# A hybrid retention and attention layer: convolution constants loaded during the retention, rotation and output gate of the retention on VectorE

## The chip, the cores and the metric

The kernel runs on one core of one Trainium2 chip. A core has a matrix engine (TensorE, PE in the views, with its weight loads as PEld), three engines for elementwise work (VectorE as DVE, ScalarE as ACT, GpSimd as POOL) and an engine that here only issues transfers (SyncE, SP). Each engine carries out its own list of instructions in order and waits on semaphores for the others; transfers are issued by an engine (rows of SPq, POOLq) and carried out by 16 DMA engines. The metric is device time of one execution in microseconds, lower is better.

## The reference

One step of a diffusion backbone with one layer, for 128 context tokens and 512 latent tokens, D_MODEL 1024, all in float32. The parts that the change touches are the retention branch (rotation of q and k, retention, normalisation, output gate) and the constants of the convolution in the feed-forward part:

```python
def rope_1d(x, pos):
    half = x.shape[-1] // 2
    ...
    x1 = x[..., :half].astype(jnp.float32)
    x2 = x[..., half:].astype(jnp.float32)
    return jnp.concatenate([x1 * cos - x2 * sin, x2 * cos + x1 * sin], axis=-1).astype(x.dtype)

def retention_branch(rq, rk, rv, rg, pos, dec_f, dec_b, s0_f, s0_b):
    B, L, _ = rq.shape
    q = rope_1d(rq.reshape(B, L, R_HEADS, R_DK).transpose(0, 2, 1, 3), pos)
    k = rope_1d(rk.reshape(B, L, R_HEADS, R_DK).transpose(0, 2, 1, 3), pos) * (R_DK ** -0.5)
    v = rv.reshape(B, L, R_HEADS, R_DV).transpose(0, 2, 1, 3)
    ...
    o_f, s_f = retention_scan(q, k, v, lg_f, s0_f)
    o_b, s_b = retention_scan(q[:, :, ::-1], k[:, :, ::-1], v[:, :, ::-1], lg_b, s0_b)
    o = rms_scale(o_f + o_b[:, :, ::-1])
    o = o.transpose(0, 2, 1, 3).reshape(B, L, RET_V)
    return jax.nn.silu(rg.astype(jnp.float32)) * o, s_f, s_b

def token_mixer(h, w_in, ...):
    z = h @ w_in
    q, k, v, rq, rk, rv, rg, ga, gr = jnp.split(z, ...)
    ...
    ya = attend_blocks(q, k_all, v_all)
    yr, s_f, s_b = retention_branch(rq, rk, rv, rg, ret_pos, dec_f, dec_b, s0_f, s0_b)
    y = jax.nn.sigmoid(ga) * (ya @ w_att_o) + jax.nn.sigmoid(gr) * (yr.astype(h.dtype) @ w_ret_o)
    return y @ w_out, (k, v, s_f, s_b)

def conv_ffn(h, w_up, conv_w, conv_b, w_down):
    u = h @ w_up
    up = jnp.pad(u, ((0, 0), (1, 1), (0, 0)))
    uc = conv_w[0] * up[:, :L] + conv_w[1] * up[:, 1:L + 1] + conv_w[2] * up[:, 2:L + 2] + conv_b
    a, g = jnp.split(uc, 2, axis=-1)
    return (jax.nn.silu(g) * a) @ w_down
```

The layer: conditioned normalisation, then attention and retention side by side on the same input, gates and one output projection, a second conditioned normalisation and the feed-forward part, a last normalisation.

## The kernel before

**Tiles and number format.** The 640 tokens are 5 tiles of 128: t=0 is the context, t=1 to 4 are latents. A float32 matmul is made of three with a reduced format (mm3, L156 to L159): both operands are split into a high part and the rest, and high x high, high x rest and rest x high are added in PSUM. A weight of 1 MB comes into one of two buffers `raw` by a transfer on the SP queue (w_raw, L132 to L134). Then w_split (L137) makes its parts by 1024 columns: ACT casts the high part (L145), DVE subtracts it from the raw weight (L150). The parts lie in a ring of eight buffers `wh`.

**Groups.** a_group (L173) computes 512 columns for all five tiles: five PSUM banks (`mm.N`), two halves of four blocks of rows, and after the second half of a tile its evac function takes the bank over. A new group can start in a bank only when the old content has been copied out.

**Order.** The scheduler of the language orders the instructions of each engine from the program text and the dependencies; it is free to put a transfer far ahead of the text around it. In some stretches the order is fixed by hand (manual_schedule). So a row of the SP queue may stand earlier than its line suggests.

**The front.** After the normalisation of the input, the keys and values of all tiles are computed (z_kv, L432) into five banks; kv_hi and kv_lo (L337 to L340) split their weight. evac_kv (L565 to L575) copies the banks out, on ACT (L566) and DVE (L571). The group of the queries follows (evac_q, L628 to L639); its weight's halves are raw.11 and raw.16, and its first matmul writes mm.16, into the bank of mm.11. The convolution constants `cw`, 4 x [128, 44] elements (three taps and a bias for 44 blocks of 128 channels), are loaded in L754 to L756 of the program text, in the attention; each of these transfers has 5632 packets of one element of 4 bytes. cw is used first in conv (L1358), in the feed-forward part.

**The retention's projections.** RK, RQ and RV are groups (L864) whose steps are interleaved with mod_rest (L243 to L303), which computes further conditioning vectors on ACT (L290) and DVE (L292). evac_rqk (L851) handles a tile of RK or RQ: ACT copies the bank to z (L854), then the rotation multiplies the swapped halves of z with the sines (two multiplies of 128x256 on POOL, L858), z with the cosines (L860, DVE) and adds both (L861, DVE). Tiles of RK are in `ret.u5.5`, of RQ in `ret.u4.4`, the swapped product in `r2k`, a ring of buffers that many helpers share.

**The retention.** retention (L978) goes over ten pairs (t, hh) of tile and half of the heads, in three steps one pair apart: ret_a transposes q and k on PE and copies them out (kt is `ret2.rkT`, L944); DVE scales the queries by the decays there (L939); ret_b makes the scores, which DVE multiplies with the decay mask (L955); ret_c multiplies with the values and keeps the result and its squares' sums (L970). When a half is done, ret_d (L972) takes the roots and multiplies all five tiles on POOL (L976). Between these steps run the steps of the gate's first group, rg0 (L1002); the second follows behind. evac_rg (L993) makes the gate of a tile: tanh on ACT (L996), one DVE operation (L997), and the multiply of the retention's result, 128x512, on POOL (L999). Behind it the merge begins, whose first gate weight is raw.131 (L1192).

Of the kernel before, what the change touches and what calls it, by code (L numbers as in the profile page):

```python
# [70 lines left out]
def hybrid_step(ctx: ExitStack, tc: tile.TileContext, a: dict, o: dict):  # L71
    nc = tc.nc
# [369 lines left out]
    with tc.manual_schedule(engines={ET.PE, ET.DVE, ET.Activation}):  # L442
# [308 lines left out]
        for _ in range(n):  # L751
            next(fill, None)
    qts[1] = qT_head(1)
    for i in range(3):  # L754
        nc.sync.dma_start(cw[:, i, :], a["conv_w"][0, i].rearrange("(c p) -> p c", p=P))
    nc.sync.dma_start(cw[:, 3, :], a["conv_b"][0].rearrange("(c p) -> p c", p=P))  # L756
# [94 lines left out]
    def evac_rqk(i):  # L851
        def f(t, ps):
            z = rqk[i][:, t, :].rearrange("p (h d) -> p h d", h=8)
            nc.scalar.copy(z.rearrange("p h d -> p (h d)"), ps)  # L854
            sw = r2k().rearrange("p (h d) -> p h d", h=8)
            for b in range(2):
                xs = z[:, :, (1 - b) * 32:(2 - b) * 32]
                nc.gpsimd.tensor_mul(sw[:, :, b * 32:(b + 1) * 32], xs,  # L858
                                     r1[:, t, 1:2, b * 32:(b + 1) * 32].to_broadcast([P, 8, 32]))
            V.tensor_mul(z, z, r1[:, t, 0:1, :].to_broadcast([P, 8, 64]))  # L860
            V.tensor_add(z, z, sw)  # L861
        return f
# [109 lines left out]
    def ret_d(hh):  # L972
        rso = rsqrt(rs2, sso[:, hh].rearrange("p t h -> p (t h)"), 4 * NT, 1.0 / P, post=0.5)
        for t in range(NT):
            ov = rvv[hh][:, :, t, :]
            nc.gpsimd.tensor_mul(ov, ov, rso[:, 4 * t:4 * t + 4].unsqueeze(2).to_broadcast([P, 4, P]))  # L976
# [16 lines left out]
    def evac_rg(g):  # L993
        def f(t, ps):
            th = r2k()
            nc.scalar.activation(th, ps, AF.Tanh, scale=0.5)  # L996
# [2 lines left out]
            nc.gpsimd.tensor_mul(ov, ov, th.rearrange("p (h d) -> p h d", h=4))  # L999
# [782 lines left out]
```

## Time and profile before

| | us |
|---|---|
| median of three runs | 1158.55 (1156.24, 1159.28, 1158.55) |
| profiled execution, whole | 1157.51 |
| its span, first to last instruction | 1155.7 |
| busy in the span: DVE, ACT | 832.4, 599.4 |
| mean granted TensorE clock | 0.995 of full |

What lies between span and time of the profiled execution is 1.81 us, around the instructions. A slice of the page's second part is 28.9 us wide. Its rows give the busy share of each engine in tenths:

```
PE   5979999999999999999999999999999999999996
DVE  4556777677968966453747738979777598589878
POOL 0042110000012410043002223011112111121012
PEclk9989999999999999999999999999999999999999
```

Busy time says where an engine works. Whether its work sets the time is told by the waits of the engine that is always busy, and by the chain of what released what. In the rows quoted below a group has its busy time in us and the mean of one in ns, then the idle time of the engine ahead of it and what ended it.

### The profile page before, as it was taken

To read this page: it belongs to the slowest core of one execution; us is meant where nothing else is said; L and a number is where in the kernel's file an instruction comes from. 1 tells how busy PE (TensorE), PEld (TensorE's weight loads), DVE (VectorE), ACT (ScalarE), POOL (GpSimd) and SP (SyncE) were. 2 spreads that over 40 slices of the span, in tenths; PEclk is the share of its full clock that TensorE was granted. 3 is DMA by queue.
4 is the path that set the end of the run, shared out by engine and by line. 5 is a ranking of instruction groups with operands and counts; after the bars stand their busy time and mean duration, and the time that the engine had idled before them with its cause. 6 is when DMAs were issued, how large, how long until landed. Compare 5 with 4: busy or idle time off the path is not lost.

```text
span 1155.7 us, 17472 instructions
## 1 busy us (share of the span) xinstructions
PE 1118.4 (97%) x6725; PEld 1007.7 (87%) x6725; DVE 832.4 (72%) x1434; ACT 599.4 (52%) x1127; POOL 190.2 (16%) x210
## 2 busy tenths in 40 slices
PE   5979999999999999999999999999999999999996
PEld 4768899999988778888999988999899899899995
DVE  4556777677968966453747738979777598589878
ACT  5345656554232425552435536668657567475463
POOL 0042110000012410043002223011112111121012
PEclk9989999999999999999999999999999999999999
DMA  9952210015765442111116947456657656666462
GB/s 311 199 151 73 73 37 23 16 37 180 262 209 168 141 147 92 37 37 37 44 67 134 297 144 199 118 144 124 134 126 160 163 94 165 129 126 163 120 127 110
DMA packets 132611, 147.92 MB, mean 128 GB/s; under 512 B 27160, under 2 KB 101992, under 8 KB 132272
## 3 DMA queue, kind: packets, MB, share of 16 engines
q1 hardware_dynamic: 103152, 115.59, 31.3%
q0 software_dynamic: 29104, 31.10, 17.0%
q8 instruction: 53, 0.87, 0.3%
q14 instruction: 30, 0.25, 0.1%
q10 hardware_dynamic: 272, 0.11, 0.0%
HBM read 115.05 MB, written 8.67 MB: 107 GB/s over the span
## 4 chain that ended last, share of the span: by engine, by line
PE 78%; DVE 10%; ACT 5%; issue 3%; DMA 2%; POOL 1%; ACTq 0%; DVEq 0%; SPq 0%; POOLq 0%
DVE mod.acc.24_3630 L292 1%; DMA weights.raw.414_10655<-in_w_down 1%; DVE x1.u1.1_6298 L1454 1%; DMA mod.wm.31_3814<-in_w_mod 1%; DMA p1q.u1.1_598<-in_k_norm_g 0%; DMA weights.raw.247_7694<-in_w_down 0%; POOL f0.s.5_3423 L976 0%; DVE ret.u4.4_3425 L861 0%; DMA const.u2.2_72<-in_b_mod 0%; DVE ret.u4.4_3425 L860 0%; DVE x1.u1.1_6298 L1503 0%; DVE x1.u1.1_6298 L1466 0%; PE mm1.mm.16_711 L157 0%; DVE weights.raw.395_10304 L1551 0%; DVE x1.u1.1_6298 L1261 0%
## 5 line engine op out<-in xcount | busy, mean ns | idle before, releaser
L817 POOL DMA_DIRECT2D spill.u2.2_2895<-f1.s.1_1160 x1 | 0.6, 597 | 129.8 <-DVE mod.u3.3_2850 L602 129.8
L1106 POOL DMA_DIRECT2D weights.wh.164_5833<-weights.raw.156_5766 x1 | 1.3, 1342 | 69.5 <-DVE f1.s.9_5177 L1145 69.5
L1591 DVE TENSOR_TENSOR t7.u4.4_6786<-t7.u4.4_6786,const.u1.1_70 128x320 f32<-128x320 f32 x10 | 4.9, 492 | 10.1 <-ACT const.u1.1_70 L1590 10.1
L913 DVE SCALAR_TENSOR_TENSOR ret2.u1.1_4178<-ret2.u1.1_4178,const.u11.11_86 64x128 f32<-64x128 f32 x24 | 6.8, 338 | 6.4 <-ACT ret2.u1.1_4178 L906 6.3
L915 DVE SCALAR_TENSOR_TENSOR ret2.u1.1_4178<-ret2.u1.1_4178,const.u11.11_86 64x128 f32<-64x128 f32 x24 | 6.6, 381 | 4.7 <-ACT ret2.u1.1_4178 L908 4.7
L582 POOL TENSOR_TENSOR p1.u1.1_604<-p1.u3.3_608,p1q.u1.1_598 128x512 f32<-128x512 f32 x1 | 1.3, 1289 | 50.7 <-DMA p1.u3.3_608<-in_rope 50.7
L150 DVE TENSOR_TENSOR weights.wh.113_4368<-weights.raw.111_4365,weights.wh.112_4367 128x1024 fp32r<-128x1024 f32 x1 | 1.2, 1226 | 10.4 <-ACT weights.wh.112_4367 L145 10.4
L157 PE MATMUL mm1.mm.16_711<-weights.wh.12_718,acts.u1.1_90 128*128 128x512 f32 x2 | 1.4, 698 | 7.2 <-ACT p1.u4.4_610 L566 7.2
L150 DVE TENSOR_TENSOR weights.wh.18_789<-weights.raw.16_786,weights.wh.17_788 128x1024 fp32r<-128x1024 f32 x1 | 1.2, 1226 | 9.8 <-ACT weights.wh.17_788 L145 9.8
L860 DVE TENSOR_TENSOR ret.u5.5_3426<-ret.u5.5_3426,ret.u1.1_3419 128x512 f32<-128x512 f32 x5 | 3.5, 690 | 6.6 <-POOL ret.r2k.6_3541 L858 2.8
L427 ACT CAST acts.u1.1_90<-f0.s.2_104 128x640 fp32r<-128x640 f32 x4 | 2.9, 728 | 9.5 <-DVE f0.s.2_104 L425 9.5
L976 POOL TENSOR_TENSOR f0.s.5_3423<-f0.s.5_3423,ret2.ny20.13_4764 128x512 f32<-128x512 f32 x5 | 6.0, 1236 | 8.0 <-DVE ret2.ny20.13_4764 L220 8.0
L157 PEld LDWEIGHTS mm1.mm.16_711<-weights.wh.12_718,acts.u1.1_90 128*128 128x128 f32 x2 | 0.6, 309 | 7.7 <-ACT p1.u4.4_610 L566 7.6
L551 ACT ACTIVATE f0.s.3_710<-f0.s.3_710,p1q.ny20.11_878 128x128 f32<-128x128 f32 x20 | 6.0, 388 | 2.5 <-DVE p1q.ny20.11_878 L218 2.5
L444 PE MATMUL aux1.aux.1_134<-const.u1.1_70,const.u2.2_72 80*128 80x80 f32 x1 | 0.4, 368 | 7.0 <-DMA const.u2.2_72<-in_b_mod 7.0
L1498 POOL TENSOR_TENSOR x1.u1.1_6298<-x1.u1.1_6298,weights.raw.422_10855 128x512 f32<-128x512 f32 x3 | 4.9, 1629 | 12.7 <-ACT x1.tm.111_10868 L1471 9.8
L145 ACT CAST weights.wh.67_3288<-weights.raw.66_3286 128x1024 fp32r<-128x1024 f32 x1 | 1.1, 1056 | 11.3 <-PE mm3.mm.8_3129 L196 11.3
L145 ACT CAST weights.wh.77_3520<-weights.raw.76_3518 128x1024 fp32r<-128x1024 f32 x1 | 1.1, 1056 | 11.2 <-PE mm3.mm.16_3386 L196 11.2
L427 ACT CAST acts.u1.1_90<-f0.s.1_103 128x640 fp32r<-128x640 f32 x4 | 2.9, 726 | 7.5 <-DVE f0.s.1_103 L425 7.4
L145 ACT CAST weights.wh.17_788<-weights.raw.16_786 128x1024 fp32r<-128x1024 f32 x1 | 1.0, 1045 | 11.0 <-DMA weights.raw.16_786<-in_w_in 11.0
L1108 DVE TENSOR_TENSOR weights.wh.152_5685<-weights.raw.151_5631,weights.wh.152_5685 128x512 fp32r<-128x512 f32 x1 | 0.7, 696 | 8.3 <-ACT weights.wh.152_5685 L1099 8.3
L1465 DVE TENSOR_TENSOR x1.u1.1_6298<-x1.u1.1_6298,gate.u1.1_6284 128x512 f32<-128x512 f32 x10 | 6.7, 681 | 0.0
(6898 smaller groups left out, 4968.0 us busy)
## 6 DMA issues: line engine op xcount, KB each, us to landing
spill.u1.1_2894<-x1.u1.1_6298 POOLq DMA_DIRECT2D x5, 512.0 KB, 3.6
xin.u1.1_102<-in_x_sample SPq DMA_DIRECT2D x4, 512.0 KB, 4.8
p0.u5.5_119<-in_w_mod SPq DMA_DIRECT2D x2, 1024.0 KB, 10.0
p0.u6.6_125<-in_w_mod SPq DMA_DIRECT2D x2, 1024.0 KB, 14.8
p0.u7.7_128<-in_w_mod SPq DMA_DIRECT2D x2, 1024.0 KB, 12.3
gate.u1.1_6284<-spill.u3.3_2896 SPq DMA_DIRECT2D x2, 1024.0 KB, 4.8
x1.u1.1_6298<-in_x_sample SPq DMA_DIRECT2D x4, 512.0 KB, 8.9
out_y_sample<-x1.u1.1_6298 SPq DMA_DIRECT2D x8, 256.0 KB, 2.0
```

Of the source, the lines that this page charges most:

```text
L145: nc.scalar.copy(hi, rv)
L292: V.scalar_tensor_tensor(d, ws[n], sc, d, op0=ALU.mult, op1=ALU.add)
L427: nc.scalar.copy(hT[0][:, k, :], xk)
L551: nc.scalar.activation(x[:, j], x[:, j], AF.Copy, scale=rstd[:, j:j + 1])
L860: V.tensor_mul(z, z, r1[:, t, 0:1, :].to_broadcast([P, 8, 64]))
L913: V.scalar_tensor_tensor(Ss[0:64, hh, st + 1, j], Ss[0:64, hh, st, j], cdsel[0:64, h:h + 1], Ss[0:64, hh, st + 1, j], op0=ALU.mult, op1=AL ...
L915: V.scalar_tensor_tensor(Ss[64:128, hh, 2 - st, j], Ss[64:128, hh, 3 - st, j], cdsel[64:128, h:h + 1], Ss[64:128, hh, 2 - st, j], op0=ALU. ...
L976: nc.gpsimd.tensor_mul(ov, ov, rso[:, 4 * t:4 * t + 4].unsqueeze(2).to_broadcast([P, 4, P]))
L1454: V.tensor_add(x1[:, t, gs], x1[:, t, gs], down_mul(ps, t, c0))
L1465: V.tensor_mul(x1[:, t, gs], x1[:, t, gs], gb[:, t == 0, gs])
L1498: eng.tensor_mul(x, x, fg[:, c0:c0 + 512])
L1591: V.tensor_sub(his[1], his[1], u3[i])
```

## The change

It has three parts. The four transfers of the convolution constants leave the attention's text and go into the retention's, behind the first ret_a; a copy on POOL from that ret_a's kt into the first columns of cw, [128, 4] elements, goes ahead of them, and since the transfers overwrite these columns, they wait for it. The rotation's multiplies (L858 of before) go from POOL to DVE, twenty of 128x256. The gate's multiplies (L999) go from POOL to DVE, ten of 128x512.

```diff
@@ -751,9 +751,6 @@
     qts[1] = qT_head(1)
-    for i in range(3):
-        nc.sync.dma_start(cw[:, i, :], a["conv_w"][0, i].rearrange("(c p) -> p c", p=P))
-    nc.sync.dma_start(cw[:, 3, :], a["conv_b"][0].rearrange("(c p) -> p c", p=P))
     for h in range(8):
@@ -855,8 +852,8 @@
             sw = r2k().rearrange("p (h d) -> p h d", h=8)
             for b in range(2):
                 xs = z[:, :, (1 - b) * 32:(2 - b) * 32]
-                nc.gpsimd.tensor_mul(sw[:, :, b * 32:(b + 1) * 32], xs,
-                                     r1[:, t, 1:2, b * 32:(b + 1) * 32].to_broadcast([P, 8, 32]))
+                V.tensor_mul(sw[:, :, b * 32:(b + 1) * 32], xs,
+                             r1[:, t, 1:2, b * 32:(b + 1) * 32].to_broadcast([P, 8, 32]))
             V.tensor_mul(z, z, r1[:, t, 0:1, :].to_broadcast([P, 8, 64]))
             V.tensor_add(z, z, sw)
@@ -975,12 +972,20 @@
+    def conv_load(after):
+        nc.gpsimd.tensor_copy(cw[:, :, 0], after)
+        for i in range(3):
+            nc.sync.dma_start(cw[:, i, :], a["conv_w"][0, i].rearrange("(c p) -> p c", p=P))
+        nc.sync.dma_start(cw[:, 3, :], a["conv_b"][0].rearrange("(c p) -> p c", p=P))
+
     def retention():
         ...
         for i in range(len(gr) + 2):
             if i < len(gr):
                 sa[i] = ret_a(*gr[i])
+            if i == 1:
+                conv_load(sa[0][2][:, :4])
             if 0 <= i - 1 < len(gr):
                 sb[i - 1] = ret_b(*gr[i - 1], sa[i - 1][0], sa[i - 1][2])
@@ -996,7 +1001,7 @@
             V.scalar_tensor_tensor(th, th, 1.0, ps, op0=ALU.add, op1=ALU.mult)
             ov = rvv[g][:, :, t, :]
-            nc.gpsimd.tensor_mul(ov, ov, th.rearrange("p (h d) -> p h d", h=4))
+            V.tensor_mul(ov, ov, th.rearrange("p (h d) -> p h d", h=4))
```

The order of PE's instructions stays as it is; of SP, POOL and DVE it changes. In the rows below, lines of the changed kernel are shifted: L855 is L858 of before, L857 and L858 are L860 and L861, L936 is L939, L952 is L955, L967 is L970, L1002 is L997, and L1004 is the gate's multiply. The numbers behind the names count buffers and differ by a few between the kernels.

On the SP queue in the front, before (const.u14.14 is cw, const.u1.1 a table of constants):

```order
L352 DMA const.u1.1_70<-in_cst 128x644
L134 DMA weights.raw.11_716<-in_w_in 128x4x512
L755 DMA const.u14.14_89<-in_conv_w 128x44x1 x3
L756 DMA const.u14.14_89<-in_conv_b 128x44x1
L134 DMA weights.raw.16_786<-in_w_in 128x4x512
L538 DMA p1q.u1.1_598<-in_q_norm_g 128x128
```

And now, where they stand in the retention; at the front raw.16 follows raw.11 directly:

```order
L134 DMA weights.raw.121_5007<-in_w_in 128x4x512
L134 DMA weights.raw.126_5077<-in_w_in 128x4x512
L978 DMA const.u14.14_89<-in_conv_w 128x44x1 x3
L979 DMA const.u14.14_89<-in_conv_b 128x44x1
L134 DMA weights.raw.131_5186<-in_w_in 128x8x256
L134 DMA weights.raw.136_5198<-in_w_in 128x8x256
```

So the four transfers moved from between the query weight's two halves to between the last half of the output gate's weights, raw.126, and the first of the merge, raw.131.

On DVE in the group of RQ, before, behind the second part of the weight raw.91:

```order
L150 TENSOR_TENSOR weights.wh.95_3867<-weights.raw.91_3860,weights.wh.94_3866 128x1024
L292 SCALAR_TENSOR_TENSOR mod.acc.24_3630<-mod.wm.30_3792,const.u4.4_79,mod.acc.24_3630 128x1024
L292 SCALAR_TENSOR_TENSOR mod.acc.33_3885<-mod.wm.32_3883,const.u4.4_79,mod.acc.33_3885 128x1024
L860 TENSOR_TENSOR ret.u4.4_3425<-ret.u4.4_3425,ret.u1.1_3419 128x512
L292 SCALAR_TENSOR_TENSOR mod.acc.24_3630<-mod.wm.30_3792,const.u4.4_79,mod.acc.24_3630 128x1024
L861 TENSOR_TENSOR ret.u4.4_3425<-ret.u4.4_3425,ret.r2k.11_3767 128x512
L860 TENSOR_TENSOR ret.u4.4_3425<-ret.u4.4_3425,ret.u1.1_3419 128x512
```

And now:

```order
L150 TENSOR_TENSOR weights.wh.95_3863<-weights.raw.91_3856,weights.wh.94_3862 128x1024
L855 TENSOR_TENSOR ret.r2k.11_3763<-ret.u4.4_3421,ret.u1.1_3415 128x8x32 x2
L292 SCALAR_TENSOR_TENSOR mod.acc.24_3626<-mod.wm.30_3788,const.u4.4_79,mod.acc.24_3626 128x1024
L857 TENSOR_TENSOR ret.u4.4_3421<-ret.u4.4_3421,ret.u1.1_3415 128x512
L855 TENSOR_TENSOR ret.r2k.12_3782<-ret.u4.4_3421,ret.u1.1_3415 128x8x32
L858 TENSOR_TENSOR ret.u4.4_3421<-ret.u4.4_3421,ret.r2k.11_3763 128x512
L855 TENSOR_TENSOR ret.r2k.12_3782<-ret.u4.4_3421,ret.u1.1_3415 128x8x32
L292 SCALAR_TENSOR_TENSOR mod.acc.24_3626<-mod.wm.30_3788,const.u4.4_79,mod.acc.24_3626 128x1024
```

The half-multiplies L855 have come in, the first two ahead of the first L292 and the others between the old rows; the weight part wh.98 follows further down in both, behind seven L292 of this stretch.

On DVE in the retention, before, where the second half of the heads has begun and ret_d of the first half (L220 is its root) runs:

```order
L220 TENSOR_SCALAR ret2.ny20.13_4764<-ret2.ny20.13_4764 128x20
L997 SCALAR_TENSOR_TENSOR ret.r2k.64_4822<-ret.r2k.64_4822,mm3.mm.39_4362 128x512
L970 TENSOR_REDUCE const.u13.13_88<-ret.r2k.65_4831 128x4
L150 TENSOR_TENSOR weights.wh.128_5079<-weights.raw.126_5076,weights.wh.127_5078 128x1024
L939 TENSOR_TENSOR ret.r2k.67_4844<-aux3.aux.53_4835,ret.u3.3_3422 128x512
L955 TENSOR_TENSOR ret.r2k.68_4851<-aux3.aux.55_4852,ret.u2.2_3421 128x2x128
```

And now:

```order
L220 TENSOR_SCALAR ret2.ny20.13_4765<-ret2.ny20.13_4765 128x20
L1002 SCALAR_TENSOR_TENSOR ret.r2k.64_4823<-ret.r2k.64_4823,mm3.mm.39_4358 128x512
L967 TENSOR_REDUCE const.u13.13_88<-ret.r2k.65_4832 128x4
L1004 TENSOR_TENSOR f0.s.5_3419<-f0.s.5_3419,ret.r2k.64_4823 128x4x128
L150 TENSOR_TENSOR weights.wh.128_5080<-weights.raw.126_5077,weights.wh.127_5079 128x1024
L936 TENSOR_TENSOR ret.r2k.67_4845<-aux3.aux.53_4836,ret.u3.3_3418 128x512
L952 TENSOR_TENSOR ret.r2k.68_4852<-aux3.aux.55_4853,ret.u2.2_3417 128x2x128
```

L1004, the gate's multiply of tile t=2, stands ahead of the weight part wh.128 and of L936; it waits for POOL's third multiply of ret_d, which writes the tile that it changes.

## The prediction

> **What bounds the kernel now.** I read first the busy time of each engine, then the list of PE's waits, and then the timelines of the engines around the two waits that the change can reach.
>
> ```profile
> PE 1118.4 (97%) x6725; PEld 1007.7 (87%) x6725; DVE 832.4 (72%) x1434; ACT 599.4 (52%) x1127; POOL 190.2 (16%) x210
> ```
>
> TensorE (PE) is busy for 97% of the span and its work isn't touched. So the change can gain only what PE waits for or runs slowly in, 37 us in all, and an engine that it relieves counts only where PE waits for it. POOL, at 16%, is no bound. In the list of PE's waits (total, count, longest in us) two rows belong to the places changed:
>
> ```profile
> PE mm1.mm.16_711 L157 <- ACT p1.u4.4_610 L566: 7.2, 1, 7.2
> ...
> PE mm3.mm.27_3855 L158 <- DVE weights.wh.98_3985 L150: 2.2, 1, 2.2
> ```
>
> The first is the first matmul of the query group. The timeline (start, length, engine, line, operation, out<-in, idle before and its releaser) leads from there back to a queue:
>
> ```profile
> 38.02 13.49 SPq L755 DMA_DIRECT2D const.u14.14_89<-in_conv_w  x3
> 51.55 3.50 SPq L756 DMA_DIRECT2D const.u14.14_89<-in_conv_b  x1
> 55.17 3.60 SPq L134 DMA_DIRECT2D weights.raw.16_786<-in_w_in  x1
> ...
> 50.12 1.22 DVE L340 TENSOR_TENSOR weights.wh.10_472<-weights.raw.2_123,weights.wh.9_471 128x1024 fp32r<-128x1024 f32 x1
> ...
> 63.78 1.04 ACT L145 CAST weights.wh.17_788<-weights.raw.16_786 128x1024 fp32r<-128x1024 f32 x1 [10.96 <-DMA weights.raw.16_786<-in_w_in]
> 64.73 0.37 ACT L566 COPY p1.u4.4_610<-mm1.mm.11_294 128x256 f32<-128x256 f32 x1
> ...
> 66.34 0.41 DVE L571 COPY p1.vt.7_618<-mm1.mm.11_294 128x256 f32<-128x256 f32 x1
> ...
> 59.31 0.39 PE L159 MATMUL mm1.mm.15_298<-weights.wh.9_471,acts.u2.2_91 128*128 128x512 f32 x1
> 66.90 0.77 PE L157 MATMUL mm1.mm.16_711<-weights.wh.12_718,acts.u1.1_90 128*128 128x512 f32 x1 [7.20 <-ACT p1.u4.4_610 L566]
> ```
>
> What the reader is to see: the SP queue spends 13.49 + 3.50 us issuing the convolution constants, which nothing needs before the feed-forward part. Behind them stands raw.16, the second half of the query weights. ACT reaches its cast early, waits 10.96 us for it, and only then runs the copy (L566) that empties the PSUM bank of mm.11; after DVE's copy (L571) PE may overwrite that bank. PE, which finished the key and value matmuls at 59.31 + 0.39 = 59.70, stands still until 66.90.
>
> **Part 1: the constants leave the front.** raw.16 takes the buffer of raw.2, free once L340 is done: 50.12 + 1.22 = 51.34. Without the issue ahead of it the load starts at about 51.4 rather than 55.17. How long it then takes lies between two other loads of the same 1 MB (KB, us from issue to landing):
>
> ```profile
> weights.raw.36_1561<-in_w_in SPq DMA_DIRECT2D x1, 1024.0 KB, 4.9
> ...
> weights.raw.11_716<-in_w_in SPq DMA_DIRECT2D x1, 1024.0 KB, 9.7
> ```
>
> raw.36 had the DMA engines nearly to itself; raw.11 went beside the constants' single-element packets. Those packets will be gone, so I take 4.9: the cast starts at about 56.4. From cast to matmul it took 66.90 − 63.78 = 3.12 us, all of it on ACT and DVE, so PE may go on at 59.5. It ends the group before at 59.70, and I leave 0.2 of the gap: **gain 7.0**. With 9.7 the cast starts at 61.1, PE at 64.3, and the gap is 4.6: gain 2.6. These are its ends, with 7.2 above.
>
> **Part 2: the clock after the gap.** The table by stretch (length; PE, PEld, DVE, ACT, POOL busy; PEclk; DMA share; GB/s) for the 5 us behind it:
>
> ```profile
> 67.00:72.00 5.00, 5.00 (x13) 3.95 (x14) 4.82 (x10) 3.43 (x10) 4.98 (x7) 0.55 0.59 210
> ```
>
> The granted clock was 0.55 there, so 5.00 x 0.45 = 2.2 us were lost. Behind the 2.2 us gap at 400 the first matmul (row in part 3) took 0.50 us, against 0.77 here. So a short gap doesn't bring the slow clock, and **2.2** more are gained if the gap is short; nothing if it stays long enough for the drop.
>
> The length from which the clock drops isn't in the trace: 2.2 us didn't, 7.2 did. The Trainium skill, "TensorE: Matmul & The Clock Gate", section "What's actually happening", speaks of an idle window of about 3.4 us after which the clock is halved. By that rule a remaining gap of 4.6 would keep the loss, and 0.2 would not; the trace agrees at both of its points.
>
> **Part 3: the rotation moves to DVE.** PE waits 2.2 us for wh.98, which DVE makes late:
>
> ```profile
> 377.01 1.28 DVE L292 SCALAR_TENSOR_TENSOR mod.acc.24_3630<-mod.wm.30_3792,const.u4.4_79,mod.acc.24_3630 128x1024 f32<-128x1024 f32 x1 [1.51 <-issue]
> ...
> 380.88 1.21 DVE L860 TENSOR_TENSOR ret.u4.4_3425<-ret.u4.4_3425,ret.u1.1_3419 128x512 f32<-128x512 f32 x1 [1.34 <-POOL ret.r2k.11_3767 L858]
> ...
> 398.88 1.21 DVE L150 TENSOR_TENSOR weights.wh.98_3985<-weights.raw.96_3982,weights.wh.97_3984 128x1024 fp32r<-128x1024 f32 x1
> ...
> 400.15 0.50 PE L158 MATMUL mm3.mm.27_3855<-weights.wh.98_3985,acts.u1.1_90 128*128 128x512 f32 x1 [2.21 <-DVE weights.wh.98_3985 L150]
> ```
>
> PE wanted wh.98 at 400.15 − 2.21 = 397.94. Between 377.01 and 398.88 DVE idles once, 1.34 us, for POOL. But its own operations are longer there. In the groups (busy us, mean ns; then idle before) the same shapes stand at two prices, the dear ones while POOL multiplies:
>
> ```profile
> L860 DVE TENSOR_TENSOR ret.u4.4_3425<-ret.u4.4_3425,ret.u1.1_3419 128x512 f32<-128x512 f32 x5 | 5.0, 1004 | 1.3 <-POOL ret.r2k.11_3767 L858 1.3
> L860 DVE TENSOR_TENSOR ret.u5.5_3426<-ret.u5.5_3426,ret.u1.1_3419 128x512 f32<-128x512 f32 x5 | 3.5, 690 | 6.6 <-POOL ret.r2k.6_3541 L858 2.8 <-POOL ret.r2k.9_3625 L858 1.3 <-POOL ret.r2k.7_3562 L858 1.3
> L292 DVE SCALAR_TENSOR_TENSOR mod.acc.33_3885<-mod.wm.34_3907,const.u4.4_79,mod.acc.33_3885 128x1024 f32<-128x1024 f32 x2 | 3.0, 1515 | 0.0
> L292 DVE SCALAR_TENSOR_TENSOR mod.acc.24_3630<-mod.wm.29_3742,const.u4.4_79,mod.acc.24_3630 128x1024 f32<-128x1024 f32 x2 | 2.5, 1274 | 0.0
> L861 DVE TENSOR_TENSOR ret.u4.4_3425<-ret.u4.4_3425,ret.r2k.12_3786 128x512 f32<-128x512 f32 x1 | 1.2, 1229 | 0.0
> L858 POOL TENSOR_TENSOR ret.r2k.13_3808<-ret.u4.4_3425,ret.u1.1_3419 128x256 f32<-128x256 f32 x2 | 2.9, 1454 | 0.0
> ```
>
> With POOL silent: L860 frees 5 x (1.004 − 0.690) = 1.6 us, six slowed L292 at 1.515 − 1.274 free 1.5 (only wm.34's group is quoted; wm.30's and wm.32's are like it), one L861 1.229 − 0.69 = 0.5, the wait for POOL 1.34. That is 4.9. Added are ten half-multiplies of RQ; the new order puts the first two ahead of the L292 of 377.01, in the 1.51 us of idle time, which leaves eight. The trace has none on DVE in this form. The nearest row is a broadcast multiply of the same size:
>
> ```profile
> L893 DVE TENSOR_TENSOR ret.r2k.24_4197<-ret.u5.5_3426,const.u12.12_87 x2: 418/418/418, 413.2 to 414.7; 128x256 f32<-128x256 f32 x2
> ```
>
> 0.418 us long, and some 0.34 from start to start where two stand back to back (half of L860's 0.690). 8 x 0.34 = 2.7. So wh.98 starts 4.9 − 2.7 = 2.2 us earlier and is ready at 400.09 − 2.2 = 397.9, when PE wants it: **gain 2.1**. The ends are 0 and 2.2. For the half-multiply itself I keep 0.34 below and POOL's 1.45 above; the price from which it turns is with the rivals. The ten of RK fall into the 6.6 us that DVE now waits there for POOL.
>
> **Part 4: the gate multiply moves to DVE.** Its ten multiplies of 128x512 cost some 0.69 each, and most stand where DVE is free: it is 28% idle over the span. One place isn't free. For t=2 of the first half, DVE's multiply needs the third of POOL's five normalising multiplies, and in the new order stands ahead of wh.128 and r2k.67 (L939):
>
> ```profile
> L976 POOL TENSOR_TENSOR f0.s.5_3423<-f0.s.5_3423,ret2.ny20.13_4764 x5: 1035/1040/2024, 501.0 to 506.0; 128x512 f32<-128x512 f32 x5
> ...
> 501.84 0.69 DVE L970 TENSOR_REDUCE const.u13.13_88<-ret.r2k.65_4831 128x4 f32<-128x512 f32 x1 [0.37 <-ACT ret.r2k.65_4831 L968]
> 503.78 1.37 DVE L150 TENSOR_TENSOR weights.wh.128_5079<-weights.raw.126_5076,weights.wh.127_5078 128x1024 fp32r<-128x1024 f32 x1 [1.25 <-ACT weights.wh.127_5078 L145]
> 505.07 0.68 DVE L939 TENSOR_TENSOR ret.r2k.67_4844<-aux3.aux.53_4835,ret.u3.3_3422 128x512 f32<-128x512 f32 x1
> ...
> 505.85 0.44 PE L963 MATMUL aux3.aux.57_4860<-f0.s.6_3424,ret.r2k.63_4801 128*128 128x128 f32 x2
> ...
> 509.32 0.60 ACT L996 ACTIVATE ret.r2k.70_4885<-mm3.mm.40_4363 128x512 f32<-128x512 f32 x1 [0.29 <-POOL f0.s.5_3423 L999]
> ```
>
> The third multiply ends near 501.03 + 3 x 1.04 = 504.15; DVE's follows and ends at 504.84, 1.06 after wh.128 could start. L939 moves with it, and PE's L963, which starts 0.1 us behind L939's end at 505.75, waits for DVE there: PE loses about 1.0. Back come the 0.3 us that ACT waited for POOL's gate multiply at 509. Net **cost 0.7**. Its ends: −0.4 (the wait falls where PE has other work, and all waits for POOL go) and +3 (the same for t=3 and t=4, one us each).
>
> The Trainium skill, same page, section "Architectural detail: the array is 16× 32×32, not 1× 128×128", calls ACT and DVE strictly first in, first out; by it nothing overtakes the waiting multiply, as counted; could L939 pass, this part would be −0.3.
>
> **Part 5: the constants in their new place.** POOL's copy waits for the first ret_a's kt:
>
> ```profile
> L944 ACT COPY ret2.rkT.4_4485<-aux3.aux.18_4482 x1: 372/372/372, 461.9 to 461.9; 128x256 f32<-128x256 f32 x1
> ...
> 474.69 0.37 SPq L134 DMA_DIRECT2D weights.raw.131_5185<-in_w_in  x1
> ...
> 528.38 1.05 ACT L145 CAST weights.wh.132_5187<-weights.raw.131_5185 128x1024 fp32r<-128x1024 f32 x1 [7.34 <-PE mm3.mm.46_5005 L158]
> ```
>
> SP issues for the same 17.0 us from about 463 to 480, and behind it only raw.131 is late, by some 5 us: at worst it lands at 480 + 9.7 = 490, and its cast at 528.38 waited for PE. The cover is 38 us: cost 0. The copy, of four columns, is shorter than any row here; between 0 and L976's 1.04 it changes nothing, since only the load waits for it.
>
> **Sum.** −7.0 − 2.2 − 2.1 + 0.7 = −10.6 on the profiled execution's 1157.51 (span 1155.7 and 1.8 around it): 1146.9, say **1147.0**. The median of the runs, 1158.55, is 1.0 above the profiled execution, so a median could be 1148.
>
> **Rivals.** *raw.16 still lands late*: with the constants gone, the small loads behind it and the rest of the front still share the DMA engines. At raw.11's 9.7 us the gap is 4.6, the gain 2.6 and, if the clock still drops, nothing of part 2: 1157.51 − 2.6 − 2.1 + 0.7 = 1153.5; without the drop 1151.3. Against it: raw.11's neighbours were the packets that go. 0.12. *The wait for POOL in the retention is dearer*, +3 in place of +0.7: 1149.3, or up to 1152 if PE falls behind again after each. 0.08. *It does not do what it says*: another load or the order holds ACT's cast just as long, and parts 1 and 2 are void: 1157.51 − 2.1 + 0.7 = 1156.1. Against it: only the constants stand between raw.11 and raw.16. 0.06. *Slower: DVE becomes the bound between 342 and 400.* Of the twenty half-multiplies at price p, four are taken up by the 6.6 us and two by the 1.51; fourteen push wh.98. For the time to pass 1161.0 they must cost 14.0 us beyond the forecast, so 14.0 / 14 + 0.34 = 1.34 us each decides. At POOL's 1.45 it is 14 x 1.11 = 15.5: 1162.5. L893's 0.418 speaks against it. 0.04.
>
> **How the numbers follow.** The forecast, 1144 to 1150, has 0.70. The range's low end is 1147 less 1.1 for part 4's low end and some 3 us for DVE operations elsewhere that POOL slows like the quoted ones and that I did not count: 1143. It reaches up to the late landing, 1154. A measurement of this kernel tells about 0.3%, 3.5 us, from no change: on the profiled execution's scale, faster is below 1154.0, slower above 1161.0. Faster holds the forecast and the first two rivals, 0.90; same the third, 0.06; slower the last, 0.04.
>
> **What would show it.** Right: raw.16 issued near 51.4; PE's wait before mm.16 under 1 us and PEclk 1.0 in 60 to 72; no wait for wh.98, half-multiplies near 0.42 and L860's successor at 0.69; the constants issued from about 452 (everything is 11 us earlier by then) with raw.131 there before its cast; one DVE wait of 1.6 us for POOL at the third gate multiply. Wrong: a gap over 3 us in the front, DVE half-multiplies over 1.3 us, or a new PE wait for a weight in 342 to 400.

## The result and the profile after

The changed kernel took 1147.95 us (median of four runs, 1147.59 to 1148.87), the kernel before 1157.59 in its four runs beside it. The ratio is 0.9917, with a 95% interval of 0.9900 to 0.9934: faster by 0.8%. The profiled execution took 1147.93 (span 1146.1), 9.58 less than that of before.

Busy time by engine, in the profile of the changed kernel:

```profile
PE 1116.3 (97%) x6725; PEld 1006.6 (88%) x6725; DVE 841.5 (73%) x1464; ACT 598.8 (52%) x1127; POOL 154.4 (13%) x181
```

DVE has 9 us more, POOL 36 us less, and neither number tells anything of the 9.6 us. PE's does a little: 2.1 us less for the same 6725 matmuls, about what the slow clock behind mm.16 had cost. The rest is in the list of PE's waits (total, count, longest):

```profile
PE aux1.aux.1_134 L444 <- DMA const.u2.2_72<-in_b_mod: 6.9, 1, 6.9
PE mm1.mm.1_161 L389 <- DVE xin.u1.1_102 L380: 5.2, 1, 5.2
PE aux3.aux.57_4861 L960 <- DVE ret.r2k.67_4845 L936: 2.2, 1, 2.2
```

The two rows of before that the prediction quoted, 7.2 at mm.16 and 2.2 at wh.98, are gone; one of 2.2 in the retention is new. The start of PE's first matmul into a bank, taken from both timelines, shows where the time went:

| PE's first matmul into | before | after | gained so far |
|---|---|---|---|
| mm.16, first of the queries | 66.90 | 59.91 | 6.99 |
| mm.17, the next tile | 71.89 | 62.74 | 9.15 |
| mm.32, behind RQ and RV | 413.65 | 401.98 | 11.67 |
| aux.57, in the retention | 505.85 | 496.56 | 9.29 |
| aux.58, the next tile there | 510.48 | 500.78 | 9.70 |
| mm7.mm.62, near the end | 1119.25 | 1109.72 | 9.53 |

So four steps, +7.0, +2.2, +2.5 and −2.0, and nothing of size between them or behind. The front in the timeline of the changed kernel (start, length, engine, line, out<-in, idle before and its releaser):

```profile
37.41 0.37 SPq L134 DMA_DIRECT2D weights.raw.11_716<-in_w_in  x1
51.71 0.37 SPq L134 DMA_DIRECT2D weights.raw.16_786<-in_w_in  x1
...
56.80 1.05 ACT L145 CAST weights.wh.17_788<-weights.raw.16_786 128x1024 fp32r<-128x1024 f32 x1 [3.68 <-DMA weights.raw.16_786<-in_w_in]
...
59.91 0.47 PE L157 MATMUL mm1.mm.16_711<-weights.wh.12_718,acts.u1.1_90 128*128 128x512 f32 x1
```

raw.16 is issued 3.46 us earlier than before (51.71 against 55.17), and its cast begins 5.09 us behind that (8.61 before). These two, 6.98 together, are what mm.16 gained. The clock behind it is whole, by the table by stretch (length; PE, PEld, DVE, ACT, POOL busy; PEclk; DMA share; GB/s):

```profile
60.00:65.00 5.00, 5.00 (x23) 4.12 (x23) 4.95 (x13) 3.35 (x10) 4.47 (x5) 1.00 0.71 244
```

DVE in the group of RQ, in the groups of the changed kernel and its timeline:

```profile
L857 DVE TENSOR_TENSOR ret.u4.4_3421<-ret.u4.4_3421,ret.u1.1_3415 128x512 f32<-128x512 f32 x5 | 3.4, 684 | 0.0
L292 DVE SCALAR_TENSOR_TENSOR mod.acc.33_3881<-mod.wm.34_3903,const.u4.4_79,mod.acc.33_3881 128x1024 f32<-128x1024 f32 x2 | 2.6, 1280 | 0.0
L855 DVE TENSOR_TENSOR ret.r2k.13_3804<-ret.u4.4_3421,ret.u1.1_3415 128x256 f32<-128x256 f32 x2 | 0.8, 418 | 0.0
```

```profile
386.22 1.22 DVE L150 TENSOR_TENSOR weights.wh.98_3981<-weights.raw.96_3978,weights.wh.97_3980 128x1024 fp32r<-128x1024 f32 x1
```

The cosine multiply went from a mean of 1004 to 684 ns, L292 from 1515 to 1280, and the half-multiply takes 418. wh.98 begins at 386.22; less the 9.15 gained up to there, that of before would stand at 389.73. It is 3.5 us earlier, and PE no longer waits.

The retention, in the same kernel's timeline:

```profile
489.34 5.48 POOL L973 TENSOR_TENSOR f0.s.5_3419<-f0.s.5_3419,ret2.ny20.13_4765 128x512 f32<-128x512 f32 x5 [38.44 <-DVE ret2.ny20.13_4765 L220]
...
492.41 1.51 DVE L1004 TENSOR_TENSOR f0.s.5_3419<-f0.s.5_3419,ret.r2k.64_4823 128x512 f32<-128x512 f32 x1 [1.58 <-POOL f0.s.5_3419 L973]
493.85 2.06 DVE L150 TENSOR_TENSOR weights.wh.128_5080<-weights.raw.126_5077,weights.wh.127_5079 128x1024 fp32r<-128x1024 f32 x1
495.82 0.68 DVE L936 TENSOR_TENSOR ret.r2k.67_4845<-aux3.aux.53_4836,ret.u3.3_3418 128x512 f32<-128x512 f32 x1
...
496.56 0.49 PE L960 MATMUL aux3.aux.57_4861<-f0.s.6_3420,ret.r2k.63_4802 128*128 128x128 f32 x2 [2.24 <-DVE ret.r2k.67_4845 L936]
```

The gate's multiply for t=2 waits 1.58 us for POOL, then takes 1.51 us instead of 0.69, wh.128 behind it 2.06 instead of 1.37, and L936, which PE's L960 needs, is late by all of it. POOL multiplies on beside them until 494.8. The other nine gate multiplies took 0.69 each.

### The profile page after: what moved, and what is told of

It is laid out like the page before. It is cut to its first block, busy times and chain, and to the rows that moved or that the text cites. A ratio compares the mean times of both kernels' runs of the same rounds, so it can differ in the third digit from the quotient of the medians.

```text
span 1146.1 us, 17450 instructions
## 1 busy us (share of the span) xinstructions
PE 1116.3 (97%) x6725; PEld 1006.6 (88%) x6725; DVE 841.5 (73%) x1464; ACT 598.8 (52%) x1127; POOL 154.4 (13%) x181
## 4 chain that ended last, share of the span: by engine, by line
PE 83%; DVE 8%; ACT 5%; issue 2%; DMA 1%; ACTq 0%; DVEq 0%; POOL 0%
DMA weights.raw.414_10656<-in_w_down 1%; DVE x1.u1.1_6299 L1459 1%; DMA weights.raw.247_7695<-in_w_down 0%; DMA const.u2.2_72<-in_b_mod 0%; DVE x1.u1.1_6299 L1508 0%; DVE x1.u1.1_6299 L1471 0%; DVE weights.raw.395_10305 L1556 0%; DVE x1.u1.1_6299 L1266 0%; DVE x1.u1.1_6299 L1466 0%; PE mm3.mm.72_6140 L1139 0%; DVE acts.u2.2_91 L430 0%; PE mm1.mm.11_294 L159 0%; PE mm7.mm.8_7506 L1582 0%; PE mm7.mm.41_9512 L1581 0%; PE mm7.mm.38_9263 L1582 0%
## 5 line engine op out<-in xcount | busy, mean ns | idle before, releaser
L973 POOL TENSOR_TENSOR f0.s.5_3419<-f0.s.5_3419,ret2.ny20.13_4765 128x512 f32<-128x512 f32 x5 | 5.5, 1124 | 38.4 <-DVE ret2.ny20.13_4765 L220 38.4
L973 POOL TENSOR_TENSOR f0.s.6_3420<-f0.s.6_3420,ret2.ny20.20_4981 128x512 f32<-128x512 f32 x5 | 5.0, 1040 | 19.7 <-DVE ret2.ny20.20_4981 L220 19.7
L145 ACT CAST weights.wh.77_3516<-weights.raw.76_3514 128x1024 fp32r<-128x1024 f32 x1 | 1.1, 1055 | 11.2 <-PE mm3.mm.16_3382 L196 11.2
L551 ACT ACTIVATE p1.u4.4_610<-p1.u4.4_610,p1.ny10.15_660 128x128 f32<-128x128 f32 x10 | 3.0, 388 | 6.5 <-DVE p1.ny10.15_660 L218 6.5
## 6 DMA issues: line engine op xcount, KB each, us to landing
p0.u7.7_128<-in_w_mod SPq DMA_DIRECT2D x2, 1024.0 KB, 12.8
```

What stands on the lines that cost most here:

```text
L145: nc.scalar.copy(hi, rv)
L551: nc.scalar.activation(x[:, j], x[:, j], AF.Copy, scale=rstd[:, j:j + 1])
```

## The experiments

Each part of the change was taken alone first. Ratios are to the kernel before, run beside each.

**Only the constants move** (rotation and gate as before):

```diff
-                V.tensor_mul(sw[:, :, b * 32:(b + 1) * 32], xs,
+                nc.gpsimd.tensor_mul(sw[:, :, b * 32:(b + 1) * 32], xs,
...
-            V.tensor_mul(ov, ov, th.rearrange("p (h d) -> p h d", h=4))
+            nc.gpsimd.tensor_mul(ov, ov, th.rearrange("p (h d) -> p h d", h=4))
```

> Only the constants' transfers move into the retention; rotation and gate stay on POOL. Theory (three independent parts; the front gave 9.15 us): PE's 7.2 us wait before mm.16 and the slow clock behind it go, the 2.2 us wait for wh.98 stays, no wait at aux.57: 1157.5 - 9.2 = 1148.3 in the profiled execution. Rival (part of the front's gain belongs to the lighter POOL): less than 8 us, over 1149.5.

1148.55 us, ratio 0.9923 (0.9904 to 0.9943); profiled 1148.32, 9.2 less than before. mm.16 starts 7.41 earlier and mm.17 9.58, the wait for wh.98 is still there (2.4), aux.57 has none. The front's gain needs neither of the other parts.

**Only the rotation moves** (the kernel before, the half-multiplies on DVE):

```diff
-                nc.gpsimd.tensor_mul(sw[:, :, b * 32:(b + 1) * 32], xs,
+                V.tensor_mul(sw[:, :, b * 32:(b + 1) * 32], xs,
```

> Only the rotation's half-multiplies move to DVE. Theory: the wait for wh.98 goes and what stands slow behind it, 2.5 us; the front's 7.2 us stay: 1155.0. Rival (wh.98 came early in the changed kernel only because everything ahead of it had shifted against the transfers): the wait stays at 1.5 to 2.5 us, 1157.0 to 1157.5.

1155.78 us, ratio 0.9980 (0.9971 to 0.9990). The profiled execution, 1157.08, had a front that was 1.3 us later than in the profile of before (7.9 us of wait at mm.16), and from there to mm.32 it gained 2.4 us; the wait for wh.98 isn't in its list. The size is that of the theory; the profiled time is not, for the front's own spread and for a wait of 1.1 us at mm7.mm.60, near the end, which the profile of before doesn't have.

**Only the gate moves** (the kernel before, the gate's multiplies on DVE):

```diff
-            nc.gpsimd.tensor_mul(ov, ov, th.rearrange("p (h d) -> p h d", h=4))
+            V.tensor_mul(ov, ov, th.rearrange("p (h d) -> p h d", h=4))
```

> Only the gate's multiplies move to DVE. Theory: PE waits about 2.2 us at aux.57 for DVE's L939, behind the gate multiply that waits for POOL's third normalising multiply; 0.4 us come back at aux.58: 1157.5 + 2.0 = 1159.5. Rival (the wait appears only with the shifted front): 1157.2, no wait over 0.5 us there.

1162.18 us, ratio 1.0033 (1.0021 to 1.0045): slower, and by more than either theory had. The wait is the 2.2 us expected; but behind it the clock fell, which it hadn't in the changed kernel. The same five us behind the gap, first of this kernel, then of the changed one:

```profile
509.00:514.00 5.00, 5.00 (x24) 4.64 (x24) 2.36 (x5) 1.81 (x4) 0.00 (x0) 0.66 0.49 154
```

```profile
497.00:502.00 5.00, 5.00 (x36) 4.37 (x35) 3.36 (x5) 2.60 (x6) 0.00 (x0) 1.00 0.53 175
```

Granted 0.66 against 1.00. From aux.57 to aux.58 it took 5.83 us here and 4.22 there, 1.6 more. Two further runs of the same kernel asked whether that is chance:

> The kernel with only the gate on DVE, a second look. In its first profile the clock fell to 0.66 behind PE's 2.2 us wait at aux.57; in the changed kernel and in three other runs the same wait of 2.2 us left it at 1.00. Theory (whether a gap of this length lowers the clock is a matter of when it falls, and differs between executions of one kernel): in two looks at least one without the drop, aux.58 then 4.2 us behind aux.57. Rival (it is fixed by this kernel's order): the drop in both, 5.8 us.

> The same as the look before it: theory, at least one of the two without the drop; rival, the drop in both.

The drop came in both: 0.66 and 0.80 in the same table, 5.82 and 5.63 us from aux.57 to aux.58. In all four kernels with this wait and the rotation on DVE (the changed one, and those without the copy, with three and with two taps in front, below) it took 4.22.

The traces tell what decides it, and it isn't the kernel. The stretches of half clock begin and end on a raster of 3.41 us: behind the front's wait the clock is 0.50 from 64.72 to 71.55 in the kernel before (two steps) and from 62.02 to 72.26 here (three), and here again from 509.16 to 512.58 (one step, and 131 steps behind 62.02). Cut into the cells of this raster, the gap lies in one cell here, and in two in the changed kernel (same table):

```profile
505.75:509.16 3.41, 1.17 (x8) 0.73 (x7) 3.41 (x5) 0.46 (x1) 1.25 (x1) 1.00 0.00 0
509.16:512.58 3.42, 3.42 (x17) 3.32 (x16) 1.31 (x2) 0.39 (x1) 0.00 (x0) 0.50 0.27 65
```

```profile
492.00:495.41 3.41, 2.31 (x14) 1.45 (x12) 3.00 (x2) 2.00 (x5) 2.82 (x3) 1.00 0.00 0
495.41:498.83 3.42, 2.27 (x18) 2.23 (x19) 2.88 (x5) 0.18 (x1) 0.00 (x0) 1.00 0.00 0
498.83:502.24 3.41, 3.41 (x22) 2.71 (x20) 2.07 (x3) 2.63 (x7) 0.00 (x0) 1.00 0.86 283
```

PE is idle for 2.24 us of the one cell here, and for 1.1 us of each of the two there. In all fourteen traces, from 25 us on, every cell at full clock in which PE was idle for 1.9 us or more was followed by one at half clock, and none was in which it was idle for 1.75 us or less; near 1.8 both occur. The three gaps with the drop begin 0.4 to 1.6 us into their cell, the four without 1.9 to 2.8. The wait of 2.2 to 2.4 us for wh.98 is in six traces, and lowered the clock in one, where 1.98 us of it fell into one cell (the constants issued by POOL, below: 0.50 from 403.23 to 406.64). The raster stands differently against the program in each execution, so by this reading it is chance that the drop went by kernel here, and the reason that the theory gave holds, though its forecast missed. All this is read off the traces; no run set the place of the raster.

**The changed kernel with the gate back on POOL**, the edit of above turned round:

> The changed kernel with the gate's multiplies back on POOL. Theory: the wait at aux.57 goes, the 0.3 us at aux.58 are back: 1147.9 - 2.0 = 1145.9, ratio to the kernel before 0.990. Rival (the time lost there is made up by other work later, or another wait of the size takes its place): 1147.5 to 1148.

1145.61 us, ratio 0.9894 (0.9879 to 0.9909); profiled 1145.56. There is no wait at aux.57, the 0.3 us at aux.58 are back. This is the best of the kernels, better than both given ones: the constants and the rotation are worth 12 us, the gate gave 2 back (2.0 at aux.58, by the profiles).

**The gate's second half alone on DVE:**

```diff
-            V.tensor_mul(ov, ov, th.rearrange("p (h d) -> p h d", h=4))
+            (V if g else nc.gpsimd).tensor_mul(ov, ov, th.rearrange("p (h d) -> p h d", h=4))
```

> The changed kernel with the gate's multiplies of the first half of the heads on POOL, those of the second half on DVE. Theory (only the first half's multiply at t=2 costs): no wait at aux.57, time as with all of them on POOL, 1145.6, within 0.5. Rival (the second half's five on DVE cost too, at the entry of the merge): 1146.5 to 1147.5.

1146.14 us, ratio 0.9894 (0.9875 to 0.9913), no wait at aux.57. It can't be told from the gate wholly on POOL: the second half's five multiplies cost nothing that shows.

**Why that multiply was long.** In the changed kernel, POOL gives the last two of its five normalising multiplies to DVE, so that it is silent when the gate's multiply begins:

```diff
-            nc.gpsimd.tensor_mul(ov, ov, rso[:, 4 * t:4 * t + 4].unsqueeze(2).to_broadcast([P, 4, P]))
+            (V if t > 2 else nc.gpsimd).tensor_mul(ov, ov, rso[:, 4 * t:4 * t + 4].unsqueeze(2).to_broadcast([P, 4, P]))
```

> The changed kernel with ret_d's normalising multiplies of tiles 3 and 4 on DVE, tiles 0 to 2 stay on POOL; so POOL is done when the gate's multiply of t=2 begins. In the order that multiply now stands also ahead of the reduce L967. Theory (the gate's multiply of 1.51 us and the weight part wh.128 of 2.06 us were long because POOL multiplied beside them): 0.69 and 1.22 us, PE's wait at aux.57 falls from 2.2 to about 1.4, 1147.1. Rival (they are long for their own operands): 1.51 and 2.06 stay, and with the reduce of 0.69 behind the multiply the wait grows to 2.9, 1148.6.

Its timeline on POOL and DVE:

```profile
489.56 3.93 POOL L973 TENSOR_TENSOR f0.s.5_3419<-f0.s.5_3419,ret2.ny20.13_4765 128x512 f32<-128x512 f32 x3 [38.43 <-DVE ret2.ny20.13_4765 L220]
...
489.92 2.68 DVE L973 TENSOR_TENSOR f0.s.5_3419<-f0.s.5_3419,ret2.ny20.13_4765 128x512 f32<-128x512 f32 x2
493.53 0.69 DVE L1004 TENSOR_TENSOR f0.s.5_3419<-f0.s.5_3419,ret.r2k.64_4823 128x512 f32<-128x512 f32 x1 [0.93 <-POOL f0.s.5_3419 L973]
494.13 0.68 DVE L967 TENSOR_REDUCE const.u13.13_88<-ret.r2k.65_4832 128x4 f32<-128x512 f32 x1
494.73 1.22 DVE L150 TENSOR_TENSOR weights.wh.128_5080<-weights.raw.126_5077,weights.wh.127_5079 128x1024 fp32r<-128x1024 f32 x1
```

With POOL done at 493.5 the same multiply takes 0.69 and wh.128 1.22, as the theory has it; the two multiplies that DVE runs beside POOL take 1.34 each. PE's wait fell to 1.6 (1.4 expected: POOL, slowed in turn, ended its third multiply 0.9 us later), and the time is 1147.09 (ratio 0.9905, 0.9889 to 0.9921). The interval doesn't tell this from the changed kernel; the rows do.

**Without the copy:**

```diff
     def conv_load(after):
-        nc.gpsimd.tensor_copy(cw[:, :, 0], after)
```

> The changed kernel without the small copy ahead of the constants' transfers; nothing then holds them, and in the order they stand between raw.11 and raw.16 again. Theory: the front's 7 us wait and its slow clock are back, the other two parts stay: 1147.9 + 9.2 = 1157.1. Rival (the place of the transfers in the queue is not what counts): 1148 to 1150.

1157.74 us, ratio 0.9998 (0.9985 to 1.0011). The transfers stand behind raw.11 again, and PE waits 7.8 us at mm.16. Where they are written in the program decides nothing; what they wait for does. The whole change is worth nothing without this copy of 0.27 us: what the rotation gains, the gate takes back.

**What of the front was the queue, and what the packets.** Three of the four transfers back in front:

```diff
     qts[1] = qT_head(1)
+    for i in range(3):
+        nc.sync.dma_start(cw[:, i, :], a["conv_w"][0, i].rearrange("(c p) -> p c", p=P))
...
-        nc.gpsimd.tensor_copy(cw[:, :, 0], after)
-        for i in range(3):
-            nc.sync.dma_start(cw[:, i, :], a["conv_w"][0, i].rearrange("(c p) -> p c", p=P))
+        nc.gpsimd.tensor_copy(cw[:, 3, :4], after)
```

> The changed kernel with the three transfers of the taps back in front, between raw.11 and raw.16; only the bias is loaded in the retention. Three quarters of the packets are in the front again, but their issue on SP (13.5 us from 38.0) ends at about 51.5, when raw.16's buffer comes free. Theory (what held raw.16 was SP's time for issuing): raw.16 starts near 51.7, takes 5.1 us, PE's wait before mm.16 stays under 0.7 us, time as of the changed kernel, 1147.9. Rival (the packets on the DMA engines make raw.16's load long, 8.6 us as before): the cast at 60.3, the wait near 3.7 us, 1151.5, or 1153.7 if the clock drops behind it.

```profile
38.52 13.11 SPq L755 DMA_DIRECT2D const.u14.14_89<-in_conv_w  x3
51.75 3.58 SPq L134 DMA_DIRECT2D weights.raw.16_786<-in_w_in  x1
...
60.51 1.04 ACT L145 CAST weights.wh.17_788<-weights.raw.16_786 128x1024 fp32r<-128x1024 f32 x1 [7.65 <-DMA weights.raw.16_786<-in_w_in]
```

My theory fell. raw.16 is issued at the same moment as in the changed kernel, 51.75 against 51.71, and still comes 8.76 us later rather than 5.09. PE waits 3.9 us and the clock behind it is 0.70 for five us; 1154.06 us, ratio 0.9968 (0.9953 to 0.9982). What the bias held up on SP was only half of the front's wait (3.5 us); the other half is packets that are still on their way. They don't stretch the load itself: from the end of its issue to the cast it takes 5.2 us here, 5.0 before and 4.7 in the changed kernel. What they stretch is its issue, 3.58 us instead of 0.37. While it lasts, 51.75 to 55.33, the trace has only packets under 512 bytes, 0.02 MB in all:

```profile
DMA packets 5575, 0.02 MB, mean 6 GB/s; under 512 B 5575, under 2 KB 5575, under 8 KB 5575
```

The traffic behind it (last number: GB/s; the one before: share of the DMA engines), first of this kernel, then of the one before, shows raw.16's bytes moving only when the small packets are through, near 56 and 59.4:

```profile
54.00:56.00 2.00, 2.00 (x11) 1.65 (x10) 1.10 (x2) 0.00 (x0) 0.00 (x0) 1.00 1.06 9
56.00:58.00 2.00, 2.00 (x11) 1.65 (x10) 0.00 (x0) 0.00 (x0) 0.00 (x0) 1.00 0.89 233
```

```profile
58.00:59.40 1.40, 1.40 (x8) 1.08 (x6) 0.00 (x0) 0.00 (x0) 0.00 (x0) 1.00 1.12 8
59.40:62.00 2.60, 0.30 (x2) 0.00 (x0) 0.00 (x0) 0.00 (x0) 0.00 (x0) 1.00 0.90 269
```

So both halves are SP held up by the constants' packets: first in issuing the bias, then in issuing raw.16. With two taps in front, and the third and the bias in the retention:

> The changed kernel with two of the three taps' transfers back in front, between raw.11 and raw.16; the third and the bias in the retention. With three, raw.16's issue itself took 3.58 us and the load landed after 8.8, since their packets were not done when it started; with two, SP is done near 47. Theory (only packets that are still waiting when raw.16 starts cost; bias alone took 8.5 us from issue to landing, 5 us behind the end of its issue): they are through near 52, raw.16 takes 5 to 6 us, PE's wait before mm.16 is under 1 us, 1148. Rival (each transfer in the front costs its share, 3.7 us of wait for three): wait near 2.5 us, 1150.5.

```profile
37.94 9.93 SPq L755 DMA_DIRECT2D const.u14.14_89<-in_conv_w  x2
52.04 0.37 SPq L134 DMA_DIRECT2D weights.raw.16_786<-in_w_in  x1
...
57.22 1.05 ACT L145 CAST weights.wh.17_788<-weights.raw.16_786 128x1024 fp32r<-128x1024 f32 x1 [3.76 <-DMA weights.raw.16_786<-in_w_in]
```

SP is done at 47.9, four us before raw.16 may start, its issue takes 0.37 again and the load 5.18. No wait at mm.16; 1148.12 us, ratio 0.9912 (0.9893 to 0.9931), as the changed kernel. By the start of mm.17, 11,264 packets in this place are nearly free (0.4 us), 16,896 cost 5.1 us, 22,528 cost 9.2.

**The constants issued by POOL** in the kernel before, at their place in the text:

```diff
-        nc.sync.dma_start(cw[:, i, :], a["conv_w"][0, i].rearrange("(c p) -> p c", p=P))
+        nc.gpsimd.dma_start(cw[:, i, :], a["conv_w"][0, i].rearrange("(c p) -> p c", p=P))
...
-    nc.sync.dma_start(cw[:, 3, :], a["conv_b"][0].rearrange("(c p) -> p c", p=P))
+    nc.gpsimd.dma_start(cw[:, 3, :], a["conv_b"][0].rearrange("(c p) -> p c", p=P))
```

> The kernel before with the constants' four transfers issued at the front by POOL in place of SP; rotation and gate as before. Theory (issuing time on SP): raw.16 starts near 51.7 and the time is that of the kernel in which only the constants move, 1148.3. Rival (22,528 packets in the front slow raw.16 whoever issues them): raw.16 takes 8 us or more, the wait before mm.16 is 3 us or more, 1151 to 1154.

1163.69 us, ratio 1.0039 (1.0025 to 1.0053): neither. POOL has nothing to do at the start, so it issued them from 1.30 us on, among the loads of the input. The stretch from 10 to 20 us, of this kernel and of the one before:

```profile
10.00:20.00 10.00, 0.00 (x0) 0.00 (x0) 3.18 (x7) 4.26 (x8) 4.92 (x3) 1.00 1.06 171
```

```profile
10.00:20.00 10.00, 7.47 (x70) 7.04 (x71) 6.69 (x21) 7.07 (x14) 2.21 (x3) 1.00 1.12 320
```

The DMA engines are as busy and move 171 GB/s instead of 320. PE's first wait, at mm.1, is 12.0 us instead of 5.2. At mm.16 PE doesn't wait, and raw.16 takes 5.18 us (64.11 to 69.29). Still PE starts mm.17 3.3 us later than before, and loses another 1.5 us up to mm.32, where the clock fell behind the wait for wh.98. The packets cost where they run, whoever issues them.

## Why the prediction came out

**Part 1, gain 7.0: measured 6.99**, and by both terms: issue at 51.71 (51.4 predicted), 5.1 us from there to the cast (4.9). The half that could have failed is the load's time. Its working took 4.9 because "those packets will be gone", and the runs with three and two taps in front show that the packets were the reason. The argument against the rival was wrong all the same: it read raw.11's 9.7 us as the work of the constants' packets. In the changed kernel raw.11 has no such neighbours and still takes 9.7:

```profile
weights.raw.11_716<-in_w_in SPq DMA_DIRECT2D x1, 1024.0 KB, 9.7
```

It comes behind the conditioning weights on the same queue (p0.u7.7, 12.8 us from issue to landing): from 37 to 41 us, 1342 of the 1349 packets are under the 2 KB of raw.11's. The bound was taken from a load with another cause.

**Part 2, gain 2.2: measured 2.16.** The clock behind mm.16 is whole, since no gap is left there. That a gap of 2.2 us leaves the clock alone, as this part argued from one place, isn't so everywhere: it fell behind such a gap in the kernel with only the gate moved, in three profiled executions of three, and gaps of 3.9 and 7.2 us brought 0.70 and 0.55. The Trainium skill, "TensorE: Matmul & The Clock Gate", section "What's actually happening", has the clock halved after an idle window of about 3.4 us; the runs agree for 3.9 and 7.2, and differ for the 2.2 us, where the drop came below that figure, with PE idle for 1.8 to 2.24 us of one cell. By the same reading it is luck that the changed kernel's own gap of 2.24 us, at aux.57, fell into two cells in its profile; the drop behind such a gap cost 1.6 us (1.4 in one of the three).

**Part 3, gain 2.1: measured 2.5.** The half-multiply took 0.42 us as the nearest row had it, the neighbours fell to the price they have with POOL silent, and the stall went. wh.98 came 3.5 us earlier, not 2.2. The weight part wh.95, with which the stretch begins, stands at 374.28 before and at 363.86 now:

```profile
374.28 1.21 DVE L150 TENSOR_TENSOR weights.wh.95_3867<-weights.raw.91_3860,weights.wh.94_3866 128x1024 fp32r<-128x1024 f32 x1
```

```profile
363.86 1.22 DVE L150 TENSOR_TENSOR weights.wh.95_3863<-weights.raw.91_3856,weights.wh.94_3862 128x1024 fp32r<-128x1024 f32 x1
```

From there to wh.98 it is 24.60 us before and 22.36 now, 2.2 less, as the sum had it. It got there with two errors that cancel: a second slow L861, which it left out, gave 0.5, and a new wait of 0.56 us for ACT's copy, ahead of an L855, took it back. (Its six slowed L292 are three at 1.76 us; the group means mix them with three at 1.27. The total is the same.) The other 1.3 us DVE had in hand at wh.95 already. They come from the group of RK, for which the prediction counted nothing: there, too, DVE had operations slowed beside POOL, in the timeline of before

```profile
358.46 1.23 DVE L861 TENSOR_TENSOR ret.u5.5_3426<-ret.u5.5_3426,ret.r2k.9_3625 128x512 f32<-128x512 f32 x1
359.62 1.76 DVE L292 SCALAR_TENSOR_TENSOR mod.acc.24_3630<-mod.wm.26_3682,const.u4.4_79,mod.acc.24_3630 128x1024 f32<-128x1024 f32 x1
```

which take 0.69 and 1.28 now. It made no more of a gain, since PE waited only 2.2 there (2.4 to 2.5 with the first slow matmul).

**Part 4, cost 0.7: measured 2.0.** The mechanism and its place were right: DVE's wait for the third multiply, 1.6 us, L936 behind it, and PE behind that. The term that was mis-sized is "DVE's follows and ends at 504.84", which priced the multiply at 0.69 and wh.128 unchanged. They took 1.51 and 2.06, 1.5 us more together, since POOL still worked on its fourth and fifth multiply beside them. Part 3 had counted this very effect as a gain; part 4 added a multiply beside POOL and didn't count it. 0.4 came back at aux.58 (0.3 predicted). No wait of that kind came for t=3 and t=4. Of the strict order on DVE, which the Trainium skill states on the page named, section "Architectural detail: the array is 16× 32×32, not 1× 128×128", the timeline is an instance: L936 stood behind the waiting multiply.

**Part 5, cost 0: measured 0.** The timeline of the changed kernel on POOL, SP and ACT:

```profile
450.63 0.27 POOL L976 COPY const.u14.14_89<-ret2.rkT.4_4481 128x4 f32<-128x4 f32 x1 [11.53 <-ACT ret2.rkT.4_4481 L941]
450.92 7.58 SPq L978 DMA_DIRECT2D const.u14.14_89<-in_conv_w  x3
458.55 3.61 SPq L979 DMA_DIRECT2D const.u14.14_89<-in_conv_b  x1
463.01 2.91 SPq L134 DMA_DIRECT2D weights.raw.131_5186<-in_w_in  x1
...
518.66 1.05 ACT L145 CAST weights.wh.132_5188<-weights.raw.131_5186 128x1024 fp32r<-128x1024 f32 x1 [7.33 <-PE mm3.mm.46_5006 L158]
```

The issue took 11.2 us instead of 17.0, and raw.131 is issued 12 us behind the copy, and its cast waits for PE as before.

**The sum.** −7.0 − 2.2 − 2.5 + 2.0 = −9.7; the profiled executions differ by 9.58. Predicted was −10.6: the gate's 1.3 too little cost, the rotation's 0.4 too little gain. Of the rivals, the dearer wait in the retention came about in part (2.0, of its 3). The late landing came only where packets were put back. That the change would not do what it says is the kernel without the copy. The slower one, DVE as the bound, had its deciding price at 1.34 us for a half-multiply; it was 0.42.

## What to carry to other kernels

Thousands of tiny packets hold up the engine that issues them and every load that it issues behind them, so they belong where no such load is near its use, held there by a dependency; the length of the issue rows and the GB/s of the stretch show them. When work moves off an engine, price the neighbours at what they take with that engine silent, and price the moved work at what it takes beside that engine where it still runs. An instruction that may wait for another engine should not stand, on an engine that works in order, ahead of one that the bottleneck needs soon.

## What the runs showed of the hardware

- Issuing the same four transfers took SP 17.0 us in the front, with the DMA engines full in the 8 us ahead (share 1.09), and 11.2 us in the retention, with a share of 0.34 in the 10.9 us ahead; the load of 1 MB behind them in the front took 3.6 us to issue with unfinished packets ahead and 0.37 without.
- DVE's multiply of 128x512 took 0.69 us alone and 1.21 to 1.51 beside a POOL multiply; POOL's own went from 1.04 in the profile of before to 1.31 (3.93 for three) beside two of DVE's.
- PE's clock goes by cells of a raster of 3.41 us that stands differently against the program in each execution: in these fourteen traces the half clock followed every cell at full clock in which PE was idle for 1.9 us or more, and none with 1.75 us or less. So a gap of 2.24 us lowered the clock in three traces and left it whole in four.
